# Modulation rows of a two-layer hybrid backbone: float32 weights on four column strips instead of split parts, blocks paired by feature halves; two q outputs written in place

## The chip, the cores and the metric

The kernel runs on one core of one Trainium2 chip. The metric is the device time of one execution in microseconds (us). TensorE (PE) does the matmuls, VectorE (DVE) and ScalarE (ACT) the element-wise work, GpSimd (POOL) small work and its own DMA queue, SyncE (SP) issues the loads of most weights. PEld is PE's weight load, which runs beside its matmuls.

## The reference

Two layers act on 1024 latent tokens (`x`) and 256 context tokens (`ctx`) of 1024 features, in float32. Each layer begins with a modulation made from two condition vectors, `c` for the latents and `c_ctx` for the context, and a weight `w_ada[l]` of 1024 x 3072:

```
def _ada(cvec, w, b):
    m = jax.nn.silu(cvec) @ w + b
    return jnp.split(m.reshape((-1, 1, m.shape[-1])), 3, axis=-1)
...
shift, scale, gate = _ada(c, w_ada[l], b_ada[l])
shift_c, scale_c, gate_c = _ada(c_ctx, w_ada[l], b_ada[l])
h_lat = _rms(x, norm_w[l]) * (1.0 + scale) + shift
h_ctx = _rms(ctx, norm_w[l]) * (1.0 + scale_c) + shift_c
...
x = x + gate * y_lat
```

Columns 0 to 1023 of `w_ada` give the shift, the next 1024 the scale, the last 1024 the gate. Layer 0's mixer projects `h` into neighbourhood attention (16 heads) and a bidirectional mLSTM (4 heads, whose q and k of the latents get a rotation), layer 1's into a bidirectional HGRN2 (16 heads). Each ends in an output projection, and the gated result is added to `x`.

## The kernel before

**Products.** TensorE's fast float32 form (f32r) keeps fewer bits, so the kernel splits an operand into `hi` (a cast, ACT, line 74) and `lo` (what is left, DVE, line 75: `split`), and makes each large product as hi x hi + hi x lo + lo x hi (`dense`, lines 127 to 129). Weights come in pieces of 128 x 512 (`wraw` as loaded, `wh` and `wl` split); the modulated, normed input is held split and transposed as `hh` and `hl`.

**Order.** Each engine runs its instructions in a fixed order that a scheduler with a simulated timeline sets when the program is built. An `issue_after` keeps a group behind one instruction. Tiles come from pools with a number of buffers for each name (ring), and a tile that takes a buffer again waits for the last reader of the old one, be it an engine or a DMA. PSUM banks carry names too (`mm`, `tr`, `ad`, `tx`, `sa`).

**Modulation.** `ada_rows` makes 512 columns of silu(c) @ w and silu(c_ctx) @ w at a time (a block), over eight k-tiles of 128 weight rows; the weights stream through PE, and the two condition vectors are the stationary operand. It loads two k-tiles with one DMA (`adar`, 512 KB). Unless `parts` is false it splits them into `adah` and `adal` and makes two f32r matmuls for each k: hi weights against four columns (`sc4`: hi and lo of both vectors, line 174), lo weights against the two hi columns (line 175). Block 0 of layer 0 uses plain float32 instead (line 177). `ada` makes blocks 0 and 1 (shift) and 2 and 3 (scale), turns every row piece of 128 into a column with a small matmul against `sel`, which also adds the hi and lo rows (line 195), and then computes `ab`, the per-feature scale and shift of both vectors. `ada_gate` makes blocks 4 and 5.

**Where it runs.** In the start stage layer 0's blocks 0 to 3 are loaded on SP's queue through six buffers, with the first two tiles of x behind block 1 and, behind block 3, a weight block and the other tiles (`x2` ...). `norm` scales the x tiles, and `mod_tr` transposes a pair of them on PE (line 239), applies `ab` (lines 247 and 249: `ntmp`) and splits into `hh` and `hl`. Then the first product runs. In the gates stage the other eight blocks (layer 0's 4 and 5, layer 1's 0 to 5) are loaded on POOL's queue through three buffers (line 164), beside the mLSTM gates and two projections.

**q stage.** Further on, each projection of layer 0 that takes part is made by seven quarter products instead of eight (`q_seven`, four outputs from seven products in sums kept in `qu` and `qv` tiles). Each product's result is added on DVE (`q_out`, line 950) into a new buffer (`ev`, two of them, in layer 0; a ring of three in layer 1), rotated where it is q or k (lines 1018 to 1021, in place, `qs` holds an intermediate), and stored to DRAM (`md`) by POOL's queue (`q_store`, line 981). `wl` and `wh` of the next product come out of the same DVE and ACT.

Of the kernel before, what the change touches and what calls it, by code (L numbers as in the profile page):

```python
# [46 lines left out]
class Prog:  # L47
# [107 lines left out]

    def ada_rows(self, l, blk, pool, parts=True):
        nc = self.nc
        wv = self.a["wada"][l].rearrange("(k p) f -> p k f", p=P)  # L160
        ps = self.ps("ad", [4, 512])
        for k in range(0, KD, 2):
            raw = self.t(pool, [P, 2, 512], F32, "adar", self.adab)
            self.last_dma = (nc.gpsimd if l or blk > 3 else nc.sync).dma_start(
                out=raw, in_=wv[:, k : k + 2, blk * 512 : (blk + 1) * 512]
            )
            if parts:
                hi = self.t(pool, [P, 2, 512], F32R, "adah", 2)
                lo = self.t(pool, [P, 2, 512], F32R, "adal", 2)
                self.split(hi, lo, raw)  # L170
            for j in range(2):
                first, last = k + j == 0, k + j == KD - 1
                if parts:
                    nc.tensor.matmul(ps, lhsT=self.sc4[:, k + j, :], rhs=hi[:, j, :], start=first, stop=False)
                    nc.tensor.matmul(ps[0:2], lhsT=self.sc4[:, k + j, 0:2], rhs=lo[:, j, :], start=False, stop=last)
                else:
                    at = nc.tensor.matmul(ps[0:2], lhsT=self.sc[:, k + j, :], rhs=raw[:, j, :], start=first, stop=last)
                    self.last_mm = at if k + j < 5 or blk == 0 else self.last_mm
        rows = self.t(pool, [4, 512], F32, "adarow", 2)
        n = 4 if parts else 2  # L180
        nc.scalar.copy(rows[0:n], ps[0:n])
        return rows[0:n]

    def ada(self, l, pool, mid=None):
        nc, a = self.nc, self.a
        ab = self.ab[l]
        pss = self.t(pool, [P, 16, 2], F32, "adass", 1)
        for blk in range(4):
            if mid and blk == 2:
                mid()  # L190
            rows = self.ada_rows(l, blk, pool, l or blk)
            p4 = self.ps("tr", [P, 4, 2])
            n = rows.shape[0]
            for m in range(4):
                nc.tensor.matmul(p4[:, m, :], lhsT=rows[:, m * P : (m + 1) * P], rhs=self.sel[0:n], start=True, stop=True)
            nc.vector.tensor_copy(pss[:, blk * 4 : blk * 4 + 4, :], p4)
        for v in range(2):

            nc.vector.tensor_tensor(out=ab[:, 1, v, :], in0=pss[:, 0:8, v], in1=self.badap[:, l, 0:8], op=ALU.add)
            nc.vector.tensor_tensor(out=ab[:, 0, v, :], in0=pss[:, 8:16, v], in1=self.badap[:, l, 8:16], op=ALU.add)  # L200
            nc.vector.scalar_tensor_tensor(
                out=ab[:, 0, v, :], in0=ab[:, 0, v, :], scalar=1.0, in1=self.normw[:, l, :], op0=ALU.add, op1=ALU.mult
            )

    def ada_gate(self, l, pool):
        nc, a = self.nc, self.a
# [738 lines left out]
    def q_keep(self, pool, tag, m):  # L945
        return self.t(pool, [P, m * 256], F32, f"{tag}{m}", self.qn * sum(x[1] == m for x in self.units))

    def q_out(self, sink, r, c, u, in0, in1, op):
        o = self.t(self.qo[0], [P, 512], F32, *self.qo[1:])[:, 0 : u[1] * 256]
        self.nc.vector.tensor_tensor(out=o, in0=in0, in1=in1, op=op)  # L950
        sink(c, r * self.half + u[0], u[1], o)

# [287 lines left out]
    def build(self):  # L1240
# [3 lines left out]
        with ExitStack() as es:  # L1244
# [69 lines left out]
            self.slabs, self.evb, self.rawb = 4, 2, 3  # L1314
            l0 = es.enter_context(ExitStack())
            mlk = l0.enter_context(tc.tile_pool(name="mlk", bufs=1))
            with self.pp.phase(ad=2, tx=2), tc.tile_pool(name="pre", bufs=2) as pool:
# [12 lines left out]
                for tt in range(NT):  # L1330
                    self.norm(xts[tt], xts[tt], pool)
                for tt in range(0, NT, 2):
                    with tc.issue_after(self.last_mm.ins) if tt == 0 else nullcontext():
                        self.mod_tr(0, [xts[tt], xts[tt + 1]], tt, pool, self.h_sink(tt * P))
                self.na_values(0, w)
            with self.pp.phase(ad=2), tc.tile_pool(name="gates", bufs=1) as pool:
                self.ml_gates(pool, mlk)
                self.adab = 3
                self.ada_gate(0, pool)
                self.ada(1, pool)  # L1340
                self.ada_gate(1, pool)
                self.na_values(1)
                self.ml_ahead("v", 0)
            with self.pp.phase(sa=4), tc.tile_pool(name="qa", bufs=1) as pool:
                self.q_open([(0, 1), (1, 2), (3, 2)], a["wab"], (self.wp, "ev", 2), (self.wp, "wraw", 3), (pool, "qs", 2), 2)
                self.a_ahead(pool)
# [321 lines left out]
```

## Time and profile before

| | us |
|---|---|
| three runs | 3472.70, 3474.56, 3475.61 |
| median | 3474.56 |
| profiled execution | 3477.65 |
| its span | 3475.9 |
| PE busy in the span | 3433.5 (99%) |
| DVE busy | 2393.0 (69%) |
| ACT busy | 1554.2 (45%) |
| POOL busy | 508.8 (15%) |

The profile is of a single execution, slightly slower than the median; 1.75 us of it lie outside the span. A row of instructions reads: line, engine, operation, output <- inputs, shape, count, then busy time, mean duration in ns, and the idle time ahead of them with what ended it. A duration of a matmul is from its start to its modelled end, and matmuls overlap, so what one costs PE is the distance to the next start. `DMA md<-ev` is the store from `ev` to `md`, `issue` is time in which nothing that the profile shows was waited for.

### The profile page before, as it was taken

What the parts mean: (1) busy time and instruction counts of PE and PEld (TensorE: products, weight loads), DVE (VectorE), ACT (ScalarE), POOL (GpSimd) and SP (SyncE); (2) the same over time, 40 slices, a digit from 0 to 9 for tenths busy, and PEclk for the clock granted to TensorE, in tenths of its full rate; (3) what the DMA queues carried; (4) which work ended last, traced back from release to release, by engine and by line L of the source; (5) the groups of instructions that cost most, each with busy time, mean ns of one, the idle gap of its engine ahead of it and who ended that gap; (6) DMA issues with size and microseconds to landing.
All of it is one profiled execution on the core that took longest, in us unless ns stands there. A gap on an engine that the chain in (4) does not pass through costs nothing.

```text
span 3475.9 us, 63362 instructions
## 1 busy us (share of the span) xinstructions
PE 3433.5 (99%) x23790; PEld 3111.0 (90%) x23790; DVE 2393.0 (69%) x5876; ACT 1554.2 (45%) x3560; POOL 508.8 (15%) x843
## 2 busy tenths in 40 slices
PE   8999999999999999999999999999999999999999
PEld 6899999999999999988879998889999999999887
DVE  7569857766666654666668766577777777777855
ACT  6532135555545534566536323444444444444431
POOL 3211111222222211211212111000000000000010
PEclk9999999999999999999999999999999999999999
DMA  8542422332222234455475332212111111121345
GB/s 256 165 158 84 124 83 54 91 87 69 81 82 79 75 99 152 128 172 159 131 238 171 101 104 97 82 31 62 62 47 52 58 58 49 52 61 53 113 149 166
DMA packets 354131, 359.62 MB, mean 103 GB/s; under 512 B 30312, under 2 KB 298792, under 8 KB 353696
## 3 DMA queue, kind: packets, MB, share of 16 engines
q1 hardware_dynamic: 309760, 246.28, 24.0%
q0 software_dynamic: 43920, 109.16, 9.2%
q8 instruction: 188, 3.08, 0.4%
q14 instruction: 119, 0.97, 0.1%
q10 hardware_dynamic: 144, 0.13, 0.0%
HBM read 271.90 MB, written 83.42 MB: 102 GB/s over the span
## 4 chain that ended last, share of the span: by engine, by line
PE 88%; issue 4%; DMA 2%; DVE 2%; ACT 1%; POOL 1%; SPq 0%; POOLq 0%; DVEq 0%; ACTq 0%
PE mm L127 15%; PE mm L128 15%; PE mm L129 15%; PE s L1144 6%; PE mm L757 3%; PE mm L759 3%; PE mm L758 3%; PE acc L709 2%; PE tr L689 2%; PE sa L127 2%; PE sa L129 2%; PE sa L128 2%; PE acc L492 2%; PE s L499 2%; PE s L1190 1%
## 5 line engine op out<-in xcount | busy, mean ns | idle before, releaser
L128 PE MATMUL mm<-wl,hh 128*128 128x256 f32 x2200 | 633.0, 288 | 4.0 <-DVE wl L75 3.7
L127 PE MATMUL mm<-wh,hh 128*128 128x256 f32 x2200 | 632.4, 288 | 4.3 <-DVE ev L950 2.7
L129 PE MATMUL mm<-wh,hl 128*128 128x256 f32 x2200 | 632.2, 288 | 0.2 <-DVE hl L75 0.2
L129 PE MATMUL mm<-hh,wl 128*128 128x512 f32 (+1 forms) x1372 | 499.7, 364 | 0.0
L128 PE MATMUL mm<-hl,wh 128*128 128x512 f32 (+1 forms) x1372 | 495.6, 361 | 0.0
L127 PE MATMUL mm<-hh,wh 128*128 128x512 f32 (+1 forms) x1372 | 495.2, 361 | 0.0
L127 PEld LDWEIGHTS mm<-wh,hh 128*128 128x128 f32 x2200 | 420.5, 191 | 12.3 <-issue 6.9
L128 PEld LDWEIGHTS mm<-wl,hh 128*128 128x128 f32 x2200 | 420.9, 191 | 9.4 <-DVE wl L75 5.0
L129 PEld LDWEIGHTS mm<-wh,hl 128*128 128x128 f32 x2200 | 420.5, 191 | 4.1 <-issue 0.8
L74 ACT CAST wh<-wraw 128x512 fp32r<-128x512 f32 x292 | 180.0, 621 | 280.1 <-PE mm L128 147.2
L128 PEld LDWEIGHTS mm<-hl,wh 128*128 128x128 f32 x1372 | 259.3, 189 | 32.2
L127 PEld LDWEIGHTS mm<-hh,wh 128*128 128x128 f32 x1372 | 259.4, 189 | 32.1
L129 PEld LDWEIGHTS mm<-hh,wl 128*128 128x128 f32 x1372 | 259.2, 189 | 32.0 <-issue 0.2
L1135 ACT COPY gksel<-gK 128x512 f32<-128x512 f32 x224 | 148.3, 663 | 275.7 <-PE s L1144 264.6
L75 DVE TENSOR_TENSOR wl<-wraw,wh 128x512 fp32r<-128x512 f32 x292 | 198.5, 688 | 50.5 <-ACT wh L74 47.9
L1144 PE MATMUL s<-gQ,gksel 128*128 128x128 f32 x1536 | 202.1, 276 | 0.0
L1144 PEld LDWEIGHTS s<-gQ,gksel 128*128 128x128 f32 x1536 | 192.6, 191 | 5.8
L757 PE MATMUL mm<-woh,yh 128*128 128x512 f32 (+1 forms) x420 | 168.9, 402 | 4.1 <-issue 2.3
L758 PE MATMUL mm<-wol,yh 128*128 128x512 f32 (+1 forms) x420 | 167.1, 399 | 0.0
L759 PE MATMUL mm<-woh,yl 128*128 128x512 f32 (+1 forms) x420 | 166.2, 397 | 0.1
L1165 DVE TENSOR_TENSOR gQ<-gQ,gT 128x256 f32<-128x256 f32 x384 | 143.9, 417 | 21.3 <-PE s L1144 21.3
L74 ACT CAST wh<-b 128x512 fp32r<-128x512 f32 x122 | 75.7, 620 | 182.3 <-PE sa L129 56.4
(551 smaller groups left out, 8240.4 us busy)
## 6 DMA issues: line engine op xcount, KB each, us to landing
wraw<-in_wc_dram SPq DMA_DIRECT2D x130, 256.0 KB
wraw<-yd SPq DMA_DIRECT2D x128, 256.0 KB
wraw<-in_wab_dram SPq DMA_DIRECT2D x98, 256.0 KB
md<-ev POOLq DMA_DIRECT2D x94, 256.0 KB, 2.7
adar<-in_wada_dram POOLq DMA_DIRECT2D x32, 512.0 KB, 5.0
b<-in_wc_dram SPq DMA_DIRECT2D x62, 256.0 KB
adar<-in_wada_dram SPq DMA_DIRECT2D x16, 512.0 KB
wraw<-in_wab_dram SPq DMA_DIRECT2D x64, 128.0 KB
```

The lines of the kernel that those rows point to most:

```text
L74: nc.scalar.copy(hi, x)
L75: nc.vector.tensor_tensor(out=lo, in0=x, in1=hi.bitcast(F32), op=ALU.subtract)
L127: mm(ps, lhsT=lh(k), rhs=rh(k), start=(first and k == 0), stop=False)
L128: mm(ps, lhsT=lh(k), rhs=rl(k), start=False, stop=False)
L129: mm(ps, lhsT=ll(k), rhs=rh(k), start=False, stop=(last and k == nk - 1))
L492: nc.tensor.matmul(num, lhsT=qc[:, j, :], rhs=C[d][:, j, :], start=False, stop=(j == 1))
L757: mm(ps, lhsT=yh[:, k, :], rhs=w.h(k)[:, cols], start=(k == 0), stop=False)
L758: mm(ps, lhsT=yh[:, k, :], rhs=w.l(k)[:, cols], start=False, stop=False)
L759: mm(ps, lhsT=yl[:, k, :], rhs=w.h(k)[:, cols], start=False, stop=(k == 7))
L1135: nc.scalar.copy(ksel.rearrange("p (b s i) -> p b s i", s=2, i=h), pick(K))
L1144: nc.tensor.matmul(pa[:, c, :].rearrange("p (b s i) -> p b s i", s=2, i=h), lhsT=ksel[:, c * P : (c + 1) * P], rhs=qp[:, c * nbc : (c + 1) ...
L1165: nc.vector.tensor_tensor(out=t[:, i, :, s, :], in0=t[:, i, :, s, :], in1=bc(tot), op=ALU.mult)
```

## The change

Modulation: there are no parts. Each k-tile takes one plain float32 matmul whose stationary operand is `scw`, the two silu vectors in the first two of 32 columns, the rest zero. It writes the PSUM partitions 32j to 32j+31 with j = k mod 4, on the column strip of the array that belongs to them; k-tiles 0 to 3 start the four strips, 4 to 7 end them. The row tile is then 128 x 512, and `sel`, with ones in rows 32j and 32j+1, adds the four strips in the same four small matmuls. `adak` is the number of k-tiles that a load carries: two in the start stage, through eight buffers, and four (1 MB) in the gates stage, through two buffers.

Blocks go in the order 0, 2, 1, 3, so that shift and scale of the first half of the features are complete after two blocks, and `ab` is computed for each half. The first two x tiles are still loaded behind two blocks. `mod_tr` of the first pair may now start behind block 2's last matmul, where it stood behind a matmul of block 3. Layer 0's transposed rows take an `mm` bank.

q stage: the outputs of the products "22" and "s4", the last that use a `u` or `v` sum, are added into that sum's own tile, rotated there and stored from there.

```
-    def ada_rows(self, l, blk, pool, parts=True):
+    def ada_rows(self, l, blk, pool):
...
-        ps = self.ps("ad", [4, 512])
-        for k in range(0, KD, 2):
-            raw = self.t(pool, [P, 2, 512], F32, "adar", self.adab)
+        ps = self.ps("ad", [P, 512])
+        m = self.adak
+        for k in range(0, KD, m):
+            raw = self.t(pool, [P, m, 512], F32, "adar", self.adab)
...
-                if parts:
-                    nc.tensor.matmul(ps, lhsT=self.sc4[:, k + j, :], rhs=hi[:, j, :], start=first, stop=False)
-                    nc.tensor.matmul(ps[0:2], lhsT=self.sc4[:, k + j, 0:2], rhs=lo[:, j, :], start=False, stop=last)
...
+            for j in range(m):
+                c = (k + j) % 4 * 32
+                self.last_mm = nc.tensor.matmul(
+                    ps[c : c + 32], lhsT=self.scw[:, k + j, :], rhs=raw[:, j, :], start=k < 4, stop=k >= 4,
+                    tile_position=(0, c),
+                )
...
-        for blk in range(4):
-            if mid and blk == 2:
+        for blk in (0, 2, 1, 3):
+            if mid and blk == 1:
                 mid()
-            rows = self.ada_rows(l, blk, pool, l or blk)
-            p4 = self.ps("tr", [P, 4, 2])
+            rows = self.ada_rows(l, blk, pool)
+            if blk == 2:
+                self.mid_mm = self.last_mm
+            p4 = self.ps("tr" if l else "mm", [P, 4, 2])
...
+            i, u = blk // 2, blk % 2
+            nc.vector.tensor_copy(pss[:, i, u], p4.rearrange("p m v -> p v m"))
+            if i:
...
-    def q_out(self, sink, r, c, u, in0, in1, op):
-        o = self.t(self.qo[0], [P, 512], F32, *self.qo[1:])[:, 0 : u[1] * 256]
+    def q_out(self, sink, r, c, u, in0, in1, op, o=None):
+        if o is None:
+            o = self.t(self.qo[0], [P, 512], F32, *self.qo[1:])[:, 0 : u[1] * 256]
...
-            self.q_out(sink, 1, 0, i, u[i], ps, ALU.add)
+            self.q_out(sink, 1, 0, i, u[i], ps, ALU.add, u[i])
...
-            self.q_out(sink, 0, 1, i, v[i], ps, ALU.add)
+            self.q_out(sink, 0, 1, i, v[i], ps, ALU.add, v[i])
...
-            self.sc4 = self.t(cp, [P, KD, 4], F32R, "sc4")
-            self.split(self.sc4[:, :, 0:2], self.sc4[:, :, 2:4], self.sc)
-            self.sel = load("sel", [4, 2])
+            self.sel = self.t(cp, [P, 2], F32, "sel")
+            nc.vector.memset(self.sel, 0.0)
+            for j in range(4):
+                nc.gpsimd.dma_start(out=self.sel[32 * j : 32 * j + 2, :], in_=a["sel"][0:2])
...
+            nc.vector.memset(self.scw, 0.0)
+            nc.vector.tensor_copy(self.scw[:, :, 0:2], self.sc)
...
-                self.adab = 6
+                self.adab, self.adak = 8, 2
...
-                self.adab = 3
+                self.adab, self.adak = 2, 4
```

The program is 148 rows shorter on PE. The first place is PE at the end of the start stage. Before, the last rows of block 3 (tile `tr_318`) are followed by the second halves of the first pair of x tiles (`x_34`, `x_35`) and by the second pair, and the first product comes at the end:

```order
L175 MATMUL ad_275<-adal_309,sc_27_107 2x512
L195 MATMUL tr_318<-sel_110,adarow_316 128x2 [waits Activation_49]
L195 MATMUL tr_318<-sel_110,adarow_316 128x2 x3
L239 MATMUL tr_432<-ident_75,x_34_139 128x128 [waits PE_49]
...
L239 MATMUL tr_472<-ident_75,x_36_141 128x128 [waits DVE_49]
...
L127 MATMUL mm_632<-wh_331,hh_128 128x256 [waits Activation_49]
```

And now, where line 190 is the small matmul (line 195 before) and line 170 the strip matmul:

```order
L190 MATMUL mm_176<-sel_107,adarow_174 128x2 x3
L190 MATMUL mm_201<-sel_107,adarow_199 128x2 x4
...
L170 MATMUL ad_237<-adar_250,scw_137 32x512 [waits DMAHW2_49]
L170 MATMUL ad_237<-adar_250,scw_137 32x512
L190 MATMUL mm_256<-sel_107,adarow_254 128x2 [waits DVE_49,Activation_49]
L190 MATMUL mm_256<-sel_107,adarow_254 128x2 x3
L127 MATMUL mm_567<-wh_266,hh_129 128x256 [waits DVE_49]
...
L239 MATMUL tr_407<-ident_75,x_36_148 128x128 [waits DVE_49]
```

The transposes of the first pair have moved ahead of block 3, and twelve products stand ahead of the second pair.

The second place is PE in the gates stage, beside the projection of the second value block (`mm`). Before, f32r records on hi and lo weights lie singly and in threes between the products:

```order
L174 MATMUL ad_1223<-adah_1256,sc_27_107 4x512
L127 MATMUL mm_1707<-wh_1528,hh_128 128x256
...
L175 MATMUL ad_1223<-adal_1257,sc_27_107 2x512
L174 MATMUL ad_1223<-adah_1256,sc_27_107 4x512
L175 MATMUL ad_1223<-adal_1257,sc_27_107 2x512
L128 MATMUL mm_1707<-wl_1539,hh_128 128x256
```

Now four strip matmuls, one load's worth, stand together, with 25 products up to the next four and 29 more up to those after:

```order
L127 MATMUL mm_1314<-wh_1251,hh_129 128x256
L170 MATMUL ad_1102<-adar_1109,scw_137 32x512 x4
L128 MATMUL mm_1314<-wl_1250,hh_129 128x256
...
L170 MATMUL ad_1123<-adar_1124,scw_137 32x512 x4
L129 MATMUL mm_1366<-wh_1251,hl_130 128x256
...
L170 MATMUL ad_1123<-adar_1130,scw_137 32x512 x4
```

A load that takes the buffer of `adar_1109` can be issued behind the first of these groups; with two buffers that is the load of `adar_1130`, 54 products and one group later.

The third place is DVE in the q stage of layer 0 (`qu` and `qv` are the sums, DMASW a store on POOL's queue). Before:

```order
L950 TENSOR_TENSOR ev_3797<-qu_511_3177,mm_3784 128x256 [waits DMASW7_49]
...
L1018 TENSOR_TENSOR qs_3799<-ev_3797,mrope_2103 128x256 [waits DVE_49]
...
L950 TENSOR_TENSOR ev_3830<-qu_513_3204,tr_3805 128x512 [waits DMASW0_49]
...
L950 TENSOR_TENSOR ev_3863<-qu_515_3231,mm_3838 128x512 [waits DMASW1_49]
L950 TENSOR_TENSOR ev_3887<-qv_576_3621,sa_3874 128x256 [waits DMASW2_49,DVE_49]
```

And now (line 951):

```order
L951 TENSOR_TENSOR ev_3482<-qv_476_3389,tr_3457 128x512 [waits DMASW1_49]
...
L951 TENSOR_TENSOR qu_409_2916<-qu_409_2916,tr_3516 128x512 [waits PE_49]
...
L1019 TENSOR_TENSOR qs_3542<-qu_409_2916,mrope_1815 128x512 [waits DVE_49]
L951 TENSOR_TENSOR qu_411_2943<-qu_411_2943,mm_3548 128x512 [waits PE_49]
...
L951 TENSOR_TENSOR qv_474_3361<-qv_474_3361,sa_3603 128x512 [waits PE_49]
```

Every add waited for a store out of `ev`; now those of the first two products of a set still do, and those into `qu` and `qv` wait for the product alone.

More of the change, by code (lines that the diff above doesn't have):

```diff
@@ L154, in rsqrt @@
         g.tensor_tensor(out=out, in0=out, in1=self.mhalf[: out.shape[0], :n], op=ALU.pow)
-    def ada_rows(self, l, blk, pool, parts=True):
+    def ada_rows(self, l, blk, pool):
         nc = self.nc
         wv = self.a["wada"][l].rearrange("(k p) f -> p k f", p=P)
-        ps = self.ps("ad", [4, 512])
-        for k in range(0, KD, 2):
-            raw = self.t(pool, [P, 2, 512], F32, "adar", self.adab)
+        ps = self.ps("ad", [P, 512])
+        m = self.adak
+        for k in range(0, KD, m):
+            raw = self.t(pool, [P, m, 512], F32, "adar", self.adab)
             self.last_dma = (nc.gpsimd if l or blk > 3 else nc.sync).dma_start(
-                out=raw, in_=wv[:, k : k + 2, blk * 512 : (blk + 1) * 512]
+                out=raw, in_=wv[:, k : k + m, blk * 512 : (blk + 1) * 512]
             )
-            if parts:
[L168 to L182, printed above, removed]
+            for j in range(m):
[4 more added lines that the diff above has]
+                )
+        rows = self.t(pool, [P, 512], F32, "adarow", 2)
+        nc.scalar.copy(rows, ps)
+        return rows
     def ada(self, l, pool, mid=None):
@@ L186, in ada @@
         ab = self.ab[l]
-        pss = self.t(pool, [P, 16, 2], F32, "adass", 1)
-        for blk in range(4):
-            if mid and blk == 2:
+        pss = self.t(pool, [P, 2, 2, 2, 4], F32, "adass", 1)
+        for blk in (0, 2, 1, 3):
+            if mid and blk == 1:
                 mid()
-            rows = self.ada_rows(l, blk, pool, l or blk)
-            p4 = self.ps("tr", [P, 4, 2])
-            n = rows.shape[0]
+            rows = self.ada_rows(l, blk, pool)
+            if blk == 2:
+                self.mid_mm = self.last_mm
+            p4 = self.ps("tr" if l else "mm", [P, 4, 2])
             for m in range(4):
[L195 to L203, printed above, removed]
+                nc.tensor.matmul(p4[:, m, :], lhsT=rows[:, m * P : (m + 1) * P], rhs=self.sel, start=True, stop=True)
+            i, u = blk // 2, blk % 2
+            nc.vector.tensor_copy(pss[:, i, u], p4.rearrange("p m v -> p v m"))
+            if i:
+                s = slice(4 * u, 4 * u + 4)
+                bc = lambda t: t.unsqueeze(1).to_broadcast([P, 2, 4])
+                nc.vector.tensor_tensor(
+                    out=ab[:, 1, :, s], in0=pss[:, 0, u], in1=bc(self.badap[:, l, 4 * u : 4 * u + 4]), op=ALU.add
+                )
+                A = ab[:, 0, :, s]
+                nc.vector.tensor_tensor(out=A, in0=pss[:, 1, u], in1=bc(self.badap[:, l, 8 + 4 * u : 12 + 4 * u]), op=ALU.add)
+                nc.vector.scalar_tensor_tensor(
+                    out=A, in0=A, scalar=1.0, in1=bc(self.normw[:, l, s]), op0=ALU.add, op1=ALU.mult
+                )
     def ada_gate(self, l, pool):
@@ L1316, in build @@
             mlk = l0.enter_context(tc.tile_pool(name="mlk", bufs=1))
+            la = l0.enter_context(ExitStack())
+            scp = la.enter_context(tc.tile_pool(name="scp", bufs=1))
+            self.scw = self.t(scp, [P, KD, 32], F32, "scw")
+            nc.vector.memset(self.scw, 0.0)
+            nc.vector.tensor_copy(self.scw[:, :, 0:2], self.sc)
             with self.pp.phase(ad=2, tx=2), tc.tile_pool(name="pre", bufs=2) as pool:
-                self.adab = 6
+                self.adab, self.adak = 8, 2
                 xts = [self.t(pool, [P, D], F32, "x0", NT) for _ in range(NT)]
@@ L1332, in build @@
                 for tt in range(0, NT, 2):
-                    with tc.issue_after(self.last_mm.ins) if tt == 0 else nullcontext():
+                    with tc.issue_after(self.mid_mm.ins) if tt == 0 else nullcontext():
                         self.mod_tr(0, [xts[tt], xts[tt + 1]], tt, pool, self.h_sink(tt * P))
@@ L1343, in build @@
                 self.ml_ahead("v", 0)
+            la.close()
             with self.pp.phase(sa=4), tc.tile_pool(name="qa", bufs=1) as pool:
```

## The prediction

> **What bounds the kernel now.** I read the page's head and its chain of work first.
>
> ```profile
> span 3475.9 us, 63362 instructions
> PE 3433.5 (99%) x23790; PEld 3111.0 (90%) x23790; DVE 2393.0 (69%) x5876; ACT 1554.2 (45%) x3560; POOL 508.8 (15%) x843
> PE 88%; issue 4%; DMA 2%; DVE 2%; ACT 1%; POOL 1%; SPq 0%; POOLq 0%; DVEq 0%; ACTq 0%
> ```
>
> TensorE is busy nearly throughout and carries 88% of the chain. So an edit pays if it takes records off PE or ends a wait of PE, and work taken from VectorE, ScalarE or the queues pays only where PE waits for it. The change touches three stages, so next comes the table of busy time by stretch.
>
> ```profile
> core 0: us, PE busy (x) PEld busy (x) DVE busy (x) ACT busy (x) POOL busy (x), PEclk, DMA share, GB/s
> 5.00:40.00 35.00, 30.44 (x112) 11.05 (x112) 21.86 (x39) 22.58 (x33) 5.15 (x13) 0.92 1.01 372
> ...
> 80.00:132.00 52.00, 52.00 (x346) 44.03 (x345) 36.30 (x54) 30.50 (x39) 11.91 (x16) 1.00 0.58 185
> 132.00:146.00 14.00, 12.53 (x89) 10.33 (x88) 10.10 (x21) 8.77 (x18) 5.28 (x7) 1.00 0.78 263
> 146.00:215.00 69.00, 69.00 (x488) 57.23 (x487) 27.67 (x48) 26.21 (x44) 14.50 (x20) 1.00 0.47 148
> ...
> 435.00:450.00 15.00, 9.82 (x61) 9.44 (x60) 11.19 (x22) 0.35 (x1) 2.79 (x5) 0.80 0.32 98
> ```
>
> From 5 to 40 us the transfers fill the DMA engines (share 1.01, 372 GB/s). From 80 to 215 us, where eight blocks of modulation rows are made, PE is full but for 132 to 146. At 435 it idles a third of the time, and the clock drops to 0.80.
>
> **Start stage, 0 to 50 us.** Here go the splits of three blocks; the loads keep their bytes.
>
> ```profile
> L75 DVE TENSOR_TENSOR adal<-adar,adah 128x1024 fp32r<-128x1024 f32 x12 | 14.5, 1219 | 7.2 <-ACT adah L74 7.1
> L74 ACT CAST adah<-adar 128x1024 fp32r<-128x1024 f32 x12 | 12.5, 1045 | 12.7 <-DMA adar<-in_wada_dram 9.0 <-PE ad L174 3.6
> ...
> 42.07 0.56 PE L127 MATMUL mm<-wh,hh 128*128 128x256 f32 x1
> ...
> 46.90 0.62 ACT L74 CAST wh<-wraw 128x512 fp32r<-128x512 f32 x1
> ...
> 48.38 0.69 DVE L75 TENSOR_TENSOR wl<-wraw,wh 128x512 fp32r<-128x512 f32 x1
> ```
>
> Those 14.5 us of DVE and 12.5 us of ACT, and the matmuls on their results, lie under the loads; at nothing. SP's queue issues the same loads, x0 and x1 still behind two blocks, and eight buffers for six only issue sooner what the full engines can't take sooner. What moves is the end. Before, the first product (42.07) follows the transposes of two pairs of x tiles; in the changed order it stands right behind the last modulation row, ahead of the second pair, since the first feature half of the first pair can be modulated after blocks 0 and 2. But the stage ends when the fourth w piece is cast (46.90) and subtracted (48.38), and ACT and DVE reach that only behind the norms of the x tiles, whose loads are issued last and land no sooner; wl is there at 49.07. By the changed row order, ACT has about 1 us less ahead of that cast, and PE has by then done some 12 products of 0.12 and 8 transposes that now follow (products go at 0.12 apiece, the chain's row below): 1 + 2.5 = **-3.5 us**. The bounds are 0 (the DMA sets the end alone) and -6 (all the waiting between 42 and 49).
>
> **Gates stage, 80 to 215 us.** Before, 64 k-tiles take two f32r matmuls each:
>
> ```profile
> L175 PE MATMUL ad<-adal,sc 128*2 128x512 f32 x64 | 25.3, 395 | 0.0
> L174 PE MATMUL ad<-adah,sc 128*4 128x512 f32 x64 | 25.2, 394 | 0.0
> ...
> 92.41 0.39 PE L175 MATMUL ad<-adal,sc 128*2 128x512 f32 x1
> ...
> 94.03 0.28 PE L127 MATMUL mm<-hh,wgh 128*128 128x256 f32 x1
> ```
>
> The mean of one is a latency; the price is the pitch. Seven such records fill 92.41 to 94.03, so 0.231 each, and 128 cost 29.6 us of full PE. They go. In their place come 64 plain float32 matmuls on strips of 32 columns. No row shows a 32-column strip. The nearest are the attention outputs, on two strips of 64 columns, and for the untiled price the layer-1 scores:
>
> ```profile
> 528.35 0.28 PE L128 MATMUL mm<-wl,hh 128*128 128x256 f32 x1
> 528.56 0.44 PE L709 MATMUL acc<-apT,avw 72*64 72x128 f32 x4
> 528.83 0.61 PE L709 MATMUL acc<-apT,avc 128*64 128x128 f32 x8
> 529.27 0.61 PE L709 MATMUL acc<-apT,avw 96*64 96x128 f32 x8
> 529.81 0.42 PE L689 MATMUL tr<-ident,aP 128*96 128x128 f32 x2
> ...
> 2399.97 1.06 PE L1144 MATMUL s<-gQ,gksel 128*128 128x128 f32 x8
> 2400.86 0.39 PE L1206 MATMUL acc<-gv,gA 128*128 128x128 f32 x2
> ```
>
> Untiled, eight records of 128 columns take 0.89 us, 0.111 each, and a float32 matmul leaves two; for 512 columns that is 0.445 a record, 0.89 a matmul. Tiled, twenty records take 529.81 - 528.35 = 1.46 less one product's 0.12, or 1.34 us. Ten pairs at 0.111 are 1.11, so two strips run side by side at full overlap, and 0.23 is left for entering and leaving. I take four strips to overlap as these two do: 16 groups of four at 0.89 are 14.2, and the changed order has them in 14 bursts, 14 x 0.23 = 3.2: 17.4 for 29.6, **-12.2 us**. The bounds are four strips not overlapping at all (64 x 0.89 + 3.2 = 60.2, +30.6) and -15.4 (bursts that cost nothing). The Trainium skill, "TensorE: Matmul & The Clock Gate", section "Measured speedup vs the span model", has three column tiles of 32 at 512 streamed columns reach 2.38 times, not 3. By that, four would reach an estimated 3.2 times, the groups would take 64 x 0.89 / 3.17 = 18.0, and the time would come out 3.8 us higher than I give; the pairs above show no such loss on two strips.
>
> The splits go too, on engines that PE does not wait for here, so they pay nothing, with one exception:
>
> ```profile
> L75 DVE TENSOR_TENSOR adal<-adar,adah 128x1024 fp32r<-128x1024 f32 x32 | 38.6, 1218 | 29.0 <-ACT adah L74 28.7 <-PE mm L129 0.3
> L74 ACT CAST adah<-adar 128x1024 fp32r<-128x1024 f32 x32 | 33.4, 1048 | 30.8 <-PE ad L174 17.6 <-DMA adar<-in_wada_dram 10.3 <-PE ad L175 2.9
> ...
> 131.95 0.12 PE mm L127
> ...
> 144.61 0.39 PE L127 MATMUL mm<-wh,hh 128*128 128x256 f32 x1 [1.38 <-ACT wh L74]
> 137.07 6.85 DMA wraw<-in_wab_dram
> ...
> adar<-in_wada_dram POOLq DMA_DIRECT2D x32, 512.0 KB, 5.0
> ...
> L164 POOL DMA_DIRECT2D adar<-in_wada_dram x2: 722/723/724, 98.0 to 99.1; - x2
> DMA to landing us min/median/max: 4.1/4.2/4.3
> ```
>
> PE waits there for a piece of w whose load was released late, by a DVE that had adal ahead of the wl subtract, and then took 6.85 us beside two adar loads. With the adal work gone the release is earlier: **-1.4 us** (0 to -1.5).
>
> The new risk is the load. A load is now 1 MB and there are two buffers, so it is issued when a group of four has run, and is wanted two groups later: some 54 to 60 products of 0.12 and one burst of 1.1 between them, 7.6 to 8.3 us. Two loads of 512 KB issued at 98.0 and 99.1 had both landed by 99.1 + 4.2 = 103.3, so 1 MB in 5.3; at the page's median of 5.0 for half as much, up to 10 if they followed one another. Nearer to the first, since the engines there are at a share of 0.47 to 0.58; a late landing stops PE with all its products queued behind the group. I allow **+2 us** over 13 such loads (0 to +13 x 2 = 26). The POOL queue carries half as many, larger issues, and the four tiny loads that fill `sel` stand at its start, under the first big loads. The wider row copy on ACT (128 partitions for 4) is the same 512 columns long: nothing. DVE's gate scans get the 38.6 us that the subtracts leave, and PE was not waiting for them. The transposed rows of blocks 0 to 3 now take an `mm` bank for `tr`; with two of them and eight columns to copy out, nothing.
>
> **Layer-0 q stage, 215 to 455 us.** Two of the four outputs of each seven products now land in their own tile.
>
> ```profile
> DVE ev L950 <- DMA md<-ev: 16.2, 10, 3.1
> PE mm L127 <- DVE ev L950: 4.8, 2, 2.7
> ...
> 356.24 0.36 PE L127 MATMUL mm<-wh,s2h 128*128 128x256 f32 x1 [2.16 <-DVE ev L950]
> ...
> 436.92 0.69 DVE L950 TENSOR_TENSOR ev<-qu,sa 128x512 f32<-128x512 f32 x1 [2.77 <-DMA md<-ev]
> ...
> 438.27 0.38 PE L128 MATMUL mm<-wl,hh 128*128 128x256 f32 x1 [2.52 <-DVE wl L75]
> ...
> 444.66 0.55 PE L127 MATMUL mm<-wh,hh 128*128 128x256 f32 x1 [2.66 <-DVE ev L950]
> ...
> 450.56 0.35 PE L127 MATMUL mm<-wh,hh 128*128 128x256 f32 x1
> ```
>
> The waits of 345 to 453 us show DVE held ten times, 16.2 us, until a store out of the two-buffer `ev` ring had ended, and PE behind it: it needs the PSUM bank that the held add would free, or a wl that is queued behind that add. The three stalls are 2.16 + 2.52 + 2.66 = 7.3 us. After the third, 28 matmuls from 444.66 to 450.56 run at 0.21 instead of 0.12, 2.5 more: 9.8 in all. In the changed order the adds of "22" and "s4" wait for PE alone, and `ev` is asked for half as often. But DVE is busy 11.19 of 15 us there, so after its waits are gone it is itself the next one late. I take **-8 us** (-3, only the third stall gone, to -9.8). What is added: the next write of a `qv` tile waits for the last store out of it, one set of products later, by the order at least 1.4 us after that store should have landed; `qu` has two sets. PE has no stall in layer 1's q stage, so its three-deep ring has nothing to give: 0.
>
> **Sum.** -3.5 - 12.2 - 1.4 + 2 - 8 = -23.1. The profiled execution took 3477.65, its span and 1.75 around it, and lies 3.1 above the median of the runs shown; from it 3454.5, from the median of 3474.56 **3451.5**. A change under 0.2%, 7 us, cannot be told from none.
>
> **Rivals.**
> (a) The two halves of a float32 matmul queue: a strip's second half holds up the next strip's first, so each k takes 0.445. Then 64 x 0.445 + 3.2 = 31.7, no gain at all in the gates: 3451.5 + 14.3 = 3465.8. The same section's page, in "Step-by-step", says that matmuls stay in program order, which would allow it; the L709 rows neither show nor exclude it. Against: twenty records as 20 halves in a chain of eleven steps would take 1.22 of the 1.34, leaving only 0.12 to enter and leave; possible, less likely.
> (b) The slower side: four strips don't overlap. Two do, by L709; nothing here shows four. Wholly in turn it is +30.6 for -12.2: 3494. With the other terms at -10.9 it turns slower when a group of four takes over (29.6 + 10.9 - 3.2) / 16 = 2.3 us, between 0.89 together and 3.56 in turn.
> (c) The 1 MB loads come late: at 9 us of landing, 13 x 1 = 13 us for the 2 allowed, and some cold matmuls behind each stop: 3463; even at about 9.8 us.
> (d) DVE sets the q stage: the stalls stay with another releaser, 3459.
>
> **How the numbers follow.** The forecast 0.60, with its own range 3444 to 3459 (terms at their near bounds); (a) 0.10, (b) 0.07, (c) 0.13, (d) 0.10. Those but (b) are faster by more than 7 us, save a part of (a) and (c) when joined with (d): faster 0.86, same 0.05, slower 0.09. The range of 3441 to 3467 takes in (a), (c) and (d), and a start stage at -6 with free bursts below.
>
> **What the changed profile would show.** A float32 group in the gates: four strips' records starting within some 10 ns, twice, 0.45 apart, about 1.1 us from the product before to the one after; if they start singly, 0.445 apart, (a) or (b) holds. PE stalls between 80 and 215 by adar's DMA: at most 2 us, else (c). No L951 add on DVE waits for md's store on "22" and "s4"; no PE gap over 2 us near 356, 438 and 444, and a full clock at 445, else (d). PE's last gap in the start ends at about 46 instead of 49. What would make it wrong above all: strips that don't overlap, and cold stretches after late loads.

## The result

The changed kernel took 3449.22 us, median of 6 runs (3446.76 to 3453.21), against 3475.43 us of the kernel before beside it (3472.70 to 3476.35): a ratio of 0.9924, 95% interval 0.9914 to 0.9935. That is 26.2 us faster; 23.1 were forecast. In a later comparison the two kernels stood at 3450.87 and 3476.52 us, 0.9922 (0.9909 to 0.9936).

The page of the changed kernel's profiled execution, which took 3446.76 us and is the fastest of its six, has in its head and its chain:

```profile
span 3445.0 us, 63198 instructions
PE 3409.9 (99%) x23790; PEld 3091.1 (90%) x23790; DVE 2342.6 (68%) x5834; ACT 1509.2 (44%) x3515; POOL 500.4 (15%) x830
PE 93%; issue 2%; DMA 2%; DVE 1%; ACT 1%; POOL 0%; SPq 0%; POOLq 0%; ACTq 0%; DVEq 0%
```

PE's records are as many as before (a float32 matmul leaves two), and 93% of the chain is PE instead of 88%. Where the time went is read from rows that mean the same work in both: the 201st projection product, the first product of layer 0's q stage, the first attention output. Each stage below runs from one of these rows to the next. Of the kernel before, the start times of PE's rows (the third stands at 528.56 in the prediction's rows):

```profile
76.15 0.28 PE L129 MATMUL mm<-wh,hl 128*128 128x256 f32 x1
...
280.44 0.28 PE L127 MATMUL sa<-wh,hh 128*128 128x256 f32 x1
```

and of the changed kernel:

```profile
71.90 0.28 PE L129 MATMUL mm<-wh,hl 128*128 128x256 f32 x1
...
261.92 0.28 PE L127 MATMUL sa<-wh,hh 128*128 128x256 f32 x1
...
498.40 0.44 PE L709 MATMUL acc<-apT,avw 72*64 72x128 f32 x4
```

So the start stage gained 4.25 us, the gates stage 18.52 - 4.25 = 14.3, and the q stage 30.16 - 18.52 = 11.6. Behind 528 us the two profiles run side by side (2947.3 and 2946.6 us to the end); why the medians differ by 26 and not by 30 is told at the end. The table by stretch, of the changed kernel:

```profile
core 0: us, PE busy (x) PEld busy (x) DVE busy (x) ACT busy (x) POOL busy (x), PEclk, DMA share, GB/s
5.00:40.00 35.00, 28.60 (x133) 13.43 (x134) 11.94 (x34) 13.76 (x26) 6.97 (x16) 0.82 1.05 389
...
80.00:132.00 52.00, 52.00 (x390) 43.65 (x389) 26.24 (x56) 22.06 (x42) 8.87 (x12) 1.00 0.65 222
132.00:146.00 14.00, 14.00 (x107) 11.91 (x109) 3.44 (x12) 3.64 (x12) 1.45 (x2) 1.00 0.22 71
...
405.00:420.00 15.00, 15.00 (x129) 15.00 (x128) 10.26 (x22) 1.82 (x4) 3.43 (x5) 1.00 0.52 159
```

The start is still filled by DMA. From 132 to 146 PE is full and DVE has 3.44 us of work where it had 10.10. The stretch from 405, which answers to 435 before, is full at full clock (1.00). One group of four strips, with the products on either side:

```profile
97.52 0.28 PE L127 MATMUL mm<-wh,hh 128*128 128x256 f32 x1
97.73 1.07 PE L170 MATMUL ad<-adar,scw 128*32 128x512 f32 x8
98.72 0.38 PE L128 MATMUL mm<-wl,hh 128*128 128x256 f32 x1
```

Eight records, the two halves of four matmuls, from 97.52 to 98.72: 1.20 less the product's 0.12, or 1.08 us.

### The profile page after: what moved, and what is told of

It reads as the page before. It is cut to its first block, busy times and chain, and to the rows that moved or that the text cites. A ratio compares the mean times of both kernels' runs of the same rounds, so it can differ in the third digit from the quotient of the medians.

```text
span 3445.0 us, 63198 instructions
## 1 busy us (share of the span) xinstructions
PE 3409.9 (99%) x23790; PEld 3091.1 (90%) x23790; DVE 2342.6 (68%) x5834; ACT 1509.2 (44%) x3515; POOL 500.4 (15%) x830
## 4 chain that ended last, share of the span: by engine, by line
PE 93%; issue 2%; DMA 2%; DVE 1%; ACT 1%; POOL 0%; SPq 0%; POOLq 0%; ACTq 0%; DVEq 0%
PE mm L129 16%; PE mm L127 16%; PE mm L128 16%; PE s L1145 6%; PE mm L759 3%; PE mm L757 3%; PE mm L758 3%; PE acc L709 2%; PE sa L129 2%; PE sa L128 2%; PE sa L127 2%; PE tr L689 2%; PE s L499 2%; PE acc L492 2%; PE s L1191 1%
## 5 line engine op out<-in xcount | busy, mean ns | idle before, releaser
L1158 DVE COPY_PREDICATED gA<-glm,s 128x512 f32<-128x512 uint8 x160 | 117.3, 733 | 55.5 <-PE s L1145 55.5
```

The lines of the kernel that those rows point to most:

```text
L1158: nc.vector.copy_predicated(A, self.lmask[:, lev - 1, :].unsqueeze(1).to_broadcast([P, 4, P]), pa)
```

## The experiments

**One strip, two strips** (one_strip, two_strips). All k-tiles on one strip, or alternately on two; the row copy and `sel` are cut to the rows that exist.

```
-                c = (k + j) % 4 * 32
+                c = 0                    # one_strip
+                c = (k + j) % 2 * 32     # two_strips
```

> The changed kernel with all k-tiles on one and the same strip of 32 columns: the same loads, the same float32 matmuls, no splits, but each waits for the one before. Theory (the gates gain comes from four strips running together): 0.86 us for each k-tile, 64 x 0.86 = 55 us instead of 14, so some 41 us more than the changed kernel, about 3490 and slower than before. Rival (the gates gained mainly because the splits left DVE and ACT): at most 10 us more than the changed kernel, 3459 or less.

Measured: 3495.47 us, 1.0047 times before (1.0029 to 1.0065). PE's rows of this kernel at one group:

```profile
106.00 0.28 PE L129 MATMUL mm<-hh,wgl 128*128 128x256 f32 x1
106.21 3.62 PE L170 MATMUL ad<-adar,scw 128*32 128x512 f32 x8
109.76 0.39 PE L127 MATMUL mm<-wh,hh 128*128 128x256 f32 x1
```

From 106.00 to 109.76 less the product's 0.12 are 3.64 us, for four matmuls that take 1.08 on four strips. Up to the 1000th product the gates stage is 41.6 us longer than the changed kernel's, where 41 were expected, and the start 7.9: from 5 to 40 us PE is busy 34.57 of 35 us there, against 28.60. With the same loads and no splits the kernel is slower than before: the gates' gain is the strips running together, and without that the change loses.

> The changed kernel with the k-tiles on two strips of 32 columns. Theory: pairs of records some 7 ns apart, 0.86 us for two k-tiles, 27.5 us instead of 13.8, so 14 us more than the changed kernel, about 3463. Rival (strips overlap less than fully, as 2.38 times for three would say): the step from one strip to two is less than half, and about 3470.

Measured: 3466.46 us, 0.9966 (0.9953 to 0.9979). Up to the 1000th product the gates stage is 16.6 us longer than the changed kernel's; 1.85 of that is a wait for a load at 118 us, so 14.8 stand against the 14 expected. The median lies between theory and rival; the groups decide for the theory. Its groups of four matmuls:

```profile
106.43 0.28 PE L128 MATMUL mm<-wl,hh 128*128 128x256 f32 x1
106.64 1.91 PE L170 MATMUL ad<-adar,scw 128*32 128x512 f32 x8
108.48 0.39 PE L129 MATMUL mm<-wh,hl 128*128 128x256 f32 x1
```

2.05 less 0.12, or 1.93 us. On one, two and four strips a group takes 3.64, 1.93 and 1.08 us: the second strip saves 1.71, two whole float32 matmuls, and the next two 0.85, one more. By these three times the strips overlap fully, and what stays is 0.2 us for each burst.

**Four buffers of 512 KB** (four_small). The same strips, but a load brings two k-tiles.

```
-                self.adab, self.adak = 2, 4
+                self.adab, self.adak = 4, 2
```

> The changed kernel with four buffers of 512 KB instead of two of 1 MB in the gates stage: the same bytes and strips, but groups of two k-tiles may come apart. By the theory each lone pair costs the same 0.86 us plus 0.23 of entering and leaving as a group of four, so the 30-odd groups of the changed order cost 10 to 16 us more in the gates stage, about 3460; if the strips of neighbouring groups still run together, about 3450.

Measured: 3461.41 us, 0.9957 (0.9940 to 0.9973), 11.2 us more than the changed kernel up to the 1000th product, without a PE stall there. A lone pair is no cheaper than four:

```profile
102.66 0.28 PE L128 MATMUL mm<-wl,hh 128*128 128x256 f32 x1
102.87 1.05 PE L170 MATMUL ad<-adar,scw 128*32 128x512 f32 x4
103.86 0.38 PE L129 MATMUL mm<-wh,hl 128*128 128x256 f32 x1
```

So the 1 MB load is part of the gain: it sets four k-tiles side by side in the row order.

**The block order** (order0123).

```
-        for blk in (0, 2, 1, 3):
-            if mid and blk == 1:
+        for blk in range(4):
+            if mid and blk == 2:
```

> The changed kernel with the blocks in the old order 0, 1, 2, 3 (the first pair of x tiles may still start behind block 2). If pairing the blocks by feature halves carries the start stage's gain, the stage ends some 3 to 4 us later than in the changed kernel, about 3452; if the dropped splits or the row of products ahead of the second pair carry it, within 1 us, about 3449.

Measured: 3455.27 us, 0.9941 (0.9927 to 0.9956). By the trace, the start stage ends 1.3 us later than in the changed kernel's first profile (201st product at 73.17 instead of 71.90), but only 0.4 later than in its second (72.72). Six profiles of kernels whose PE rows are the changed kernel's up to there have that product between 71.7 and 73.9, so this one lies among them: the pairing of the blocks has no worth here that can be told from chance, and not the 3 to 4 us. The first product, at 42.07 before and 35.33 in the changed kernel, comes at 38.94: pairing brings the first product forward, but at the stage's end that is made up while PE waits for the other x tiles. Against the changed kernel's second profile this one loses 0.5 us more in the gates stage and 2.7 behind the first attention output; what makes up those 2.7 stays open.

**The q outputs alone** (q_only). The kernel before with only the two in-place outputs.

```
+        if o is None:
+            o = self.t(self.qo[0], [P, 512], F32, *self.qo[1:])[:, 0 : u[1] * 256]
...
+            self.q_out(sink, 1, 0, i, u[i], ps, ALU.add, u[i])
...
+            self.q_out(sink, 0, 1, i, v[i], ps, ALU.add, v[i])
```

> The kernel before with only the two q outputs in place; modulation as before. Theory (the three stages gain on their own, and the q stage gained by losing the waits for stores out of ev): the three PE stalls of 2 to 3 us at 356, 438 and 444 us and the slow clock behind the last are gone, no stall takes their place, and the time is 10 to 12 us below before, about 3464. Rival (the q stage gained because the shorter gates stage changed what collides there): the stalls stay in part, and less than 5 us are gained.

Measured: 3467.79 us, 0.9972 (0.9961 to 0.9983), 8.3 us by the medians, less than the 10 to 12 expected. By the trace, of an execution 2.5 us faster than that median, it is 11.8 us ahead at the first attention output, 10.8 of them from the q stage. DVE's waits for stores fall from 16.2 us to 0.6, and no stall of PE is left in the q stage. But the scheduler has set another order of DVE's rows here too, so this run does not show which of the two ended the stalls. Of this kernel, these waits (341 to 450 us) and the stretches around the first and the last two stalls:

```profile
DVE ev L951 <- DMA md<-ev: 0.6, 2, 0.3
```

```profile
345.00:360.00 15.00, 15.00 (x128) 15.00 (x128) 14.88 (x32) 2.85 (x5) 4.01 (x6) 1.00 0.49 160
420.00:440.00 20.00, 20.00 (x171) 20.00 (x170) 14.47 (x31) 4.47 (x8) 4.43 (x7) 1.00 0.48 153
```

**The modulation alone** (ada_only). The changed kernel with the two outputs through `ev` again.

```
-            self.q_out(sink, 1, 0, i, u[i], ps, ALU.add, u[i])
+            self.q_out(sink, 1, 0, i, u[i], ps, ALU.add)
...
-            self.q_out(sink, 0, 1, i, v[i], ps, ALU.add, v[i])
+            self.q_out(sink, 0, 1, i, v[i], ps, ALU.add)
```

> The changed kernel without the in-place outputs; modulation as changed. Theory: start and gates stage as in the changed kernel, 18 us below before, about 3457; the q stage loses its 7 to 10 us again, with DVE waiting for md's stores. Rival (the q stage gained from the gates stage): the q stage has lost its stalls here too, about 3447.

Measured: 3451.62 us, 0.9926 (0.9908 to 0.9944). The q stage has no stall here either, and is as short as in the changed kernel. The theory fell: the edit to the outputs is worth 10.8 us of the q stage on the kernel before, and nothing on the changed modulation. But `ev` and its stores are as before, so what ended the stalls? Two later runs, side by side (after_again and ada_again), settled that it is so:

> The changed kernel again, beside the next one: 3449 us within 3, and no PE stall between 50 and 460 us.

> The changed kernel without the in-place outputs, beside the changed one. If the in-place outputs are worth nothing once the planner's order has moved, the two agree within 3 us and neither has a PE stall in layer 0's q stage; if they keep the worth that the prediction gave them, this one is 8 to 10 us slower.

Measured: 3450.87 us (0.9922, 0.9909 to 0.9936) and, without the in-place outputs, 3450.61 us (0.9924, 0.9911 to 0.9936); neither has a stall of PE in the q stage. In the second one's trace, the waits and DVE's rows at the place that answers to 437 us of the kernel before:

```profile
DVE ev L951 <- DMA md<-ev: 7.1, 6, 2.3
```

```profile
405.24 0.42 DVE L951 TENSOR_TENSOR ev<-qu,sa 128x256 f32<-128x256 f32 x1 [1.75 <-DMA md<-ev]
...
406.50 0.69 DVE L75 TENSOR_TENSOR wl<-wraw,wh 128x512 fp32r<-128x512 f32 x1
407.10 0.68 DVE L951 TENSOR_TENSOR ev<-qu,sa 128x512 f32<-128x512 f32 x1
...
408.10 0.69 DVE L75 TENSOR_TENSOR wl<-wraw,wh 128x512 fp32r<-128x512 f32 x1
411.01 0.69 DVE L951 TENSOR_TENSOR ev<-qu,sa 128x512 f32<-128x512 f32 x1
```

Of the kernel before, the two `wl` subtracts on either side of the add that waited 2.77 us at 436.92:

```profile
433.46 0.69 DVE L75 TENSOR_TENSOR wl<-wraw,wh 128x512 fp32r<-128x512 f32 x1 [0.30 <-ACT wh L74]
...
437.53 0.69 DVE L75 TENSOR_TENSOR wl<-wraw,wh 128x512 fp32r<-128x512 f32 x1
```

In the kernel without the in-place outputs DVE still waits for stores, and for 1.75 us once. But its order is another: the first `wl` subtract of the next product stands ahead of the first long add, and the second (408.10) behind a long add that did not wait, where in the kernel before the second (437.53) stood behind the add that a store held. Only the stages ahead differ, so the scheduler, whose simulated times of the q stage move with them, must have ordered DVE's rows anew. The waits are shorter too, 7.1 us for 16.2, so this trace alone does not tell order from length. From it came theory O: not the waits cost PE time, but what is queued behind a waiting add in the order. Four kernels tested it.

**Seven buffers in the start stage** (seven_bufs).

```
-                self.adab = 6
+                self.adab = 7
```

> The kernel before with seven buffers instead of six for the loads of the start stage: no work changes, but the planner sets another order of DVE's rows in layer 0's q stage. In it the two wl subtracts of the last products stand together ahead of the adds that wait for stores, while around the first stall (356 us) the order is that of before. Theory O (the place of the wl subtracts and the PSUM-freeing adds behind a waiting add decides the stalls): the stalls at 438 and 444 us and the slow clock behind them are gone, that at 356 us stays at 2 to 3 us, and the q stage is 6 to 9 us shorter; the time 6 to 9 us below before. Rival S (the waits for stores cost PE the same in any order): 7 us of stalls stay, time as before.

Measured: 3472.89 us, 0.9990 (0.9981 to 0.9999). In the trace both expected things are there. PE's row at the first stall and DVE's at the last ones:

```profile
358.18 0.36 PE L127 MATMUL mm<-wh,s2h 128*128 128x256 f32 x1 [2.06 <-DVE ev L950]
```

```profile
431.24 0.68 DVE L75 TENSOR_TENSOR wl<-wraw,wh 128x512 fp32r<-128x512 f32 x1
432.18 0.68 DVE L950 TENSOR_TENSOR ev<-qu,sa 128x512 f32<-128x512 f32 x1
432.77 0.68 DVE L75 TENSOR_TENSOR wl<-wraw,wh 128x512 fp32r<-128x512 f32 x1
436.82 0.69 DVE L950 TENSOR_TENSOR ev<-qu,sa 128x512 f32<-128x512 f32 x1 [0.84 <-DMA md<-ev]
437.43 1.29 DVE L75 TENSOR_TENSOR wl<-wraw,wh 128x512 fp32r<-128x512 f32 x2
```

The first stall stands, PE has no further one over 0.4 us in the q stage, and that stage is 6.3 us shorter, as expected. The time is not: 3.6 us by the medians, where 6 to 9 were expected. By the trace the start stage became 1.6 us longer and the gates stage 0.4, which takes a part of it.

**Gate blocks in plain float32** (gate_f32). On the kernel before, untiled.

```
-            rows = self.ada_rows(l, blk, pool)
+            rows = self.ada_rows(l, blk, pool, False)
...
+            nc.tensor.matmul(psg, lhsT=self.sel[0:2], rhs=rows, start=True, stop=True)
```

> The kernel before with the four gate blocks (two of each layer) in plain float32, untiled, without parts; the other blocks split as before, outputs through ev. The planner's order of DVE's rows in the q stage is then near that of the changed kernel without in-place outputs. Theory: in the gates stage 32 k-tiles take 0.86 us instead of 0.46, 12.8 us more; in the q stage no stall of PE over 1 us, 10 to 12 us less; the time within 4 us of before. Rival S: 7 us or more of stalls stay in the q stage, the time 8 to 13 us above before.

Measured: 3483.34 us, 1.0021 (1.0011 to 1.0030). The gates stage lost 15.0 us, more than the 12.8 expected, and the start 1.3; the q stage gained 10.9. So the time came out 6.8 us above before, between the two expectations, and the q stage decides for the theory. This kernel's waits from 365 to 475 us and its table for most of the q stage:

```profile
DVE ev L950 <- DMA md<-ev: 11.6, 9, 3.2
...
PE mm L127 <- ACT ev L565: 0.2, 1, 0.2
```

```profile
372.00:455.00 83.00, 83.00 (x701) 83.00 (x700) 65.17 (x133) 15.11 (x25) 14.91 (x23) 1.00 0.38 118
```

This is the clearest row of the study: nine waits of DVE for stores, up to 3.2 us long, and PE, full in the table, loses nothing.

**Layer 1's blocks ahead of layer 0's gate blocks** (blocks_moved), in the kernel before.

```
-                self.ada_gate(0, pool)
                 self.ada(1, pool)
+                self.ada_gate(0, pool)
```

> The kernel before, with layer 1's four blocks made ahead of layer 0's gate blocks; the same work, splits and q outputs, but the planner sets another order of DVE's rows in layer 0's q stage. Theory O (the stalls of the q stage come from that order: a wl subtract that PE needs stands behind an add that waits for a store): here both wl of a product stand ahead of such an add, the stalls at 356, 438 and 444 us are gone, PE's idle time from 215 to 455 us falls from 7.3 to under 3 us, and the time is 5 to 12 us below before. Rival S (the waits for stores cost PE this much in any order, as the prediction had it): 7 us or more of stalls stay, and the time is that of before.

Measured: 3476.41 us, 0.9999 (0.9989 to 1.0008). The three old stalls are gone, as theory O had it, but there is a new one of 3.92 us, and the time is not lower as it should have been:

```profile
351.64 0.55 PE L127 MATMUL tr<-wh,hh 128*128 128x256 f32 x1 [3.92 <-DVE qu L974]
```

The add that PE waits for (at 350.81) did not stand behind a wait: DVE works without a pause from 343.99 us until it is done, and no longer wait for a store than 0.57 us stands ahead of it in the q stage. So theory O as it was put covers the stalls that went, and not this one, which comes of the order without such a wait. By the first attention output 3.2 us are gained in the trace and 2.3 of them lost again behind it, and the medians show none. A new order moves the stalls; it need not end them.

**One buffer of 1 MB** (one_buf), and outputs through `ev`.

```
-                self.adab, self.adak = 2, 4
+                self.adab, self.adak = 1, 4
```

> The changed kernel without in-place outputs, and with one buffer of 1 MB in the gates stage. The groups of four then stand 65 rows apart, 7.6 us of products from the group that frees the buffer to the one that needs it, and the order of DVE's rows in the q stage is near that of the kernel before again. If 1 MB lands in under 7 us, the gates stage has no stall (theory); if it takes 9, about 1.4 us for each of 15 loads, 20 us more (rival c of the prediction). In the q stage theory O expects the stalls of the kernel before back, 7 to 10 us, so about 3459; if the stalls went with the splits instead, about 3451.

Measured: 3485.22 us, 1.0032 (1.0023 to 1.0042). No group of the gates stage waits for its load by more than 0.25 us, so 7.6 us are enough for 1 MB. The q stage is where it lost, and far more than expected: it is 20.5 us longer than in the kernel before. The longest of its stalls:

```profile
308.79 0.58 PE L127 MATMUL tr<-wh,hh 128*128 128x256 f32 x1 [6.31 <-ACT hh L74]
```

With its loads spread out the last gate block ends at 216 us instead of 177, and DVE stands 17.2 us at the add of its gate row (until 220.67), with the q stage's sums queued behind. That this backlog makes the later stalls is likely, but was not tested by itself, so this kernel neither bears theory O out nor refutes it.

## Why the prediction was right, and where it was not

**The start, -3.5:** -4.3, and -3.4 in a second profile of the changed kernel (after_again). The mechanism is the one described, with other sizes. PE's last wait over 0.1 us in the start, before and in the changed kernel, and the changed kernel's cast of the fourth w piece (46.90 before):

```profile
49.13 0.39 PE L128 MATMUL mm<-wl,hh 128*128 128x256 f32 x1 [1.01 <-DVE wl L75]
...
46.38 0.39 PE L129 MATMUL mm<-wh,hl 128*128 128x256 f32 x1 [0.30 <-DVE hl L75]
...
45.80 0.61 ACT L74 CAST wh<-wraw 128x512 fp32r<-128x512 f32 x1
```

The cast comes 1.1 us earlier, as forecast, but the wait ends 2.7 earlier, and PE has done 7 more products and 8 more transposes by then (26 and 40 for 19 and 32), where 12 and 8 more were forecast. That the pairing of the blocks carries any of it is not shown: without it (order0123) the wait ends at 46.15, and PE has done 19 products and 32 transposes by then, as before.

**The matmuls of the gates, -12.2:** right, and by its own steps. Twelve bursts of 1.08 to 1.19 and two of about 2.0 make 17.2 us; 17.4 were forecast. Rivals (a) and (b) fell: four strips start 7 ns apart, and the price of not overlapping, which the prediction had at +42.8 for the whole, was measured on one strip at 41.6 in this stage. The Trainium skill's 2.38 times for three column tiles ("TensorE: Matmul & The Clock Gate", "Measured speedup vs the span model") gave an estimate of 18.0 us, to which the prediction added the bursts' entry and exit. Here 3.64 against 1.08 us is 3.4 times with entry and exit included. If the estimate of 3.2 times is taken for the whole in the same way, the trace is near it, 17.2 us for 18.0; no run here shows which way the figure is meant.

**The wait for w, -1.4:** gone, as forecast.

**The 1 MB loads, +2:** nothing. Issued to landed they took:

```profile
DMA to landing us min/median/max: 5.4/6.0/9.9
```

within the 7.6 to 8.3 us, but for the slowest, and no group waited in this kernel. Rival (c) fell. This term makes 2.0 of the 2.7 us by which the gates stage gave more (14.3 for 11.6); 0.5 more lie behind the 1000th product.

**The q stage, -8:** the size was 11.6 in the trace, beyond the bound of -9.8, and the reason was wrong for this kernel. Followed product by product, 2.6, 2.8 and 5.5 us of it lie around the three stalls and 0.7 ahead of them. The step that failed is "Two of the four outputs of each seven products now land in their own tile", taken as the cause of the whole gain. The stalls end with the in-place outputs (q_only), but they end as well in the order that the scheduler sets once the stages ahead have moved (ada_only, ada_again), and after that the outputs add nothing. The prediction took PE's 7.3 us of stalls for the price of DVE's 16.2 us of waits for stores; gate_f32 has 11.6 us of such waits and no stall. That PE's price is set by what stands behind the wait on DVE was in its own rows (`wl` at 438.27) and was not followed to its end. Rival (d), DVE as the next bound, did not come.

**The sum.** The stages gave 30.2 us in the two profiles, the medians 26.2. The profiled executions are not the median ones: that of the kernel before took 2.2 us more than the median of its six runs, that of the changed kernel 2.5 less. The second profile of the changed kernel (after_again), 3450.69 us, lies close to its median. In it the stages give 29.3 us, and behind them 2.4 are given back, mostly at the head of layer 1, in the norm of an x tile. There a one-column POOL instruction takes 2.67 us, and PE waits:

```profile
1833.80 2.67 POOL L152 TENSOR_SCALAR nr<-nss 128x1 f32<-128x1 f32 x1 [3.13 <-ACT nx L225]
...
1840.21 1.03 PE L239 MATMUL tr<-ident,nx 128*128 128x128 f32 x4 [1.85 <-DVE ntmp L249]
```

In the first profile the same instruction took 0.32 us and PE did not wait:

```profile
1831.22 0.32 POOL L152 TENSOR_SCALAR nr<-nss 128x1 f32<-128x1 f32 x1 [3.14 <-ACT nx L225]
```

The kernel before has the long POOL row too (2.66 us at 1862), but only 0.93 us of stall behind it. The same PE rows around this place, the slow matmuls behind the stall included, take 9.0 us in the changed kernel's first profile, 10.2 in the kernel before, and 12.6 to 12.7 in after_again, ada_only and order0123. The long row alone does not make the stall: ada_again has it too, and there PE waits for nothing over 0.3 us and takes 9.4:

```profile
1835.84 2.67 POOL L152 TENSOR_SCALAR nr<-nss 128x1 f32<-128x1 f32 x1 [3.13 <-ACT nx L225]
```

Why the row is long in most executions, and why it stops PE in some, stays open. So the forecast of 3451.5 came as near as it did partly by luck: in the profile near the median the stages were some 6 us better than summed, and a place that stood in no term gave back about 2.4 of them.

## What to carry to other kernels

In these kernels a wait on an engine that isn't the bound cost what was queued behind it in that engine's order, and not its own length: before pricing it, find in the order the next result that the bounding engine needs. Where a scheduler sets the order from simulated times, a change anywhere ahead can remove or make stalls further on, so a gain there is only the edit's own when the edit alone, and the change without it, have both been run; here some 11 us were to be had from either of two parts, and not twice. Narrow float32 matmuls on separate column strips paid when they came in full groups: a pair left alone cost as much as four.

## What had not been expected of the hardware

Four strips of 32 columns with 512 streamed columns each lost nothing to one another, as the prediction had taken it from two wider strips: 0.86 us for four matmuls of 0.86, beside 0.2 us for each burst. Not expected at all was a POOL instruction on a single column that takes 0.18 to 0.75 us in most of its rows and 2.67 us at one place in 12 of the 14 profiles. Where PE waits behind it as in after_again, the place costs 3.6 us more than in the profile in which it is short.
